# SwiGLU gate and up in a decoder trunk: the weight block in place of the tokens as the operand that is held

## The chip, the cores and the metric

The kernel runs on one core of one Trainium2 chip. The metric is the device time of one execution in microseconds (us). Shown is the median of three runs; a profile of one further execution says where the time goes. PE is TensorE (matmul), PEld its weight-load path, DVE VectorE, ACT ScalarE, POOL GpSimd, SP SyncE. A matmul has a stationary operand (up to 128 columns, loaded first) and a moving one (up to 512 columns); the columns of the stationary operand become the partitions of the result, and the moving columns lie along its free axis.

## The reference

The trunk has two layers over 256 tokens of width 1024. Each layer is feed-forward, token mixer (an RG-LRU block in the first layer, attention on a shared K and V in the second), feed-forward, each with a norm before and after. So there are four feed-forward parts (FFNs), and the change concerns them:

```python
def rms_norm(x, g):
    return x * lax.rsqrt(jnp.mean(x * x, axis=-1, keepdims=True) + EPS) * g

def swiglu(x, w_gate, w_up, w_down):            # 1024 -> 2816 -> 1024
    return (jax.nn.silu(x @ w_gate) * (x @ w_up)) @ w_down

f = swiglu(rms_norm(h, pre_g), w_gate, w_up, w_down)
h = h + 0.5 * rms_norm(f, post_g)
```

All inputs and the output are float32.

## The kernel before, in words

**Splitting.** Each float32 operand is split into an upper part that TensorE's fp32r format holds and the rest (`split`, lines 166 to 179: ACT writes `whi` at line 175, DVE writes `wlo` at line 176). Each product is three fp32r matmuls: upper by upper, upper by lower, lower by upper (`mm3`, lines 181 to 185).

**Items.** The work on weights is a list of items. An item's `prep` loads 512 KB of weights on SP's queue (`load_raw`, line 155; five buffers `raw`) and splits them (nine buffers each of `whi` and `wlo`); its `work` does the matmuls, once for each half t of the tokens (0 to 127 and 128 to 255). The function `run` (line 342) lets half 0 lead half 1 by 4 to 7 items; `slot` (line 333) does one piece and calls `tick`, which issues deferred work and prepares items ahead, when a running count of TensorE's work says that their load has landed.

**Gate and up** (`ffn_items`, line 453). For each of five blocks of 512 features, `proj_items` (line 357) makes four items for the gate and four for up. An item has two blocks k of 128 input features. For each k and t the stationary operand is the token block `xhi` or `xlo` (128 input features by 128 tokens), and 512 weight columns move. So the sums in PSUM (`mm`, four banks in turn) have tokens on partitions. `pair_items` (line 392) does the last 256 features of gate and up together. After a gate, ACT forms silu with the token's scale `rs[t]`, one number to a partition (line 467). After an up, DVE multiplies by silu and the scale into `prod` (line 476). Two ticks later `hidden_T` turns the product with four TensorE transposes (line 482), since the down projection needs features on partitions, and ACT and DVE split it into `hhi` and `hlo` (lines 486 and 487), one pair of tiles for each half.

**Down** (`row_items`, line 414): 22 items; the stationary operand is a block of `hhi` or `hlo`, 512 weight columns move, and two sums of 512 columns arise per half. `enter` (line 244) then normalizes, adds to the stream `h`, transposes it (line 214) and writes the next `xhi` and `xlo`; `stat` (line 239) finds the next scale `rs[t]`.

**Elsewhere.** The recurrent projection (`add_rec_units`, line 629) already holds weight blocks of 126 (the last 84) columns and moves all 256 tokens, through `mm3w` (lines 187 to 192). PE's instructions stand in the order in which they are written; the other engines' instructions are put in order by priority. Tiles lie in pools one behind another, so a tile's start depends on the sizes of those before it.

Of the kernel before, what the change touches and what calls it, by code (L numbers as in the profile page):

```python
# [9 lines left out]
F32 = mybir.dt.float32  # L10
# [6 lines left out]
P = 128  # L17
# [27 lines left out]
def trunk_kernel(ctx: ExitStack, tc: tile.TileContext, A: dict, out: bass.AP):  # L45
# [12 lines left out]
    def nm(s):  # L58
        uid[0] += 1
        return f"{s}_{uid[0]}"  # L60
# [78 lines left out]
    xhi = hpool.tile([P, 8, S], F32R, name="xhi")  # L139
    xlo = hpool.tile([P, 8, S], F32R, name="xlo")  # L140
# [96 lines left out]
    rs = [None, None]  # L237

    def stat(t):
        ss = new_ss()  # L240
        square_sum(h[t], ss[:, 0:1])
        rs[t] = rstd_of(ss, 1)

    def enter(t, dests, pf, gb, half, last=False, normed=False):

        f = 1.0 / 16 if half else 1.0 / 32
# [6 lines left out]
        for n in range(2):  # L253
            t1.append(hpool.tile([P, 512], F32, tag="t1", name=nm("t1"), bufs=2))
            nc.vector.tensor_tensor(t1[n], pf[n], gb[:, n * 512:(n + 1) * 512], ALU.mult)  # L255
        r = rstd_of(ss, 2, f)
# [9 lines left out]
        def inputs():  # L266
            tps = [to_tp(h[t], n) for n in range(2)]
            for dest in dests:
                to_x(tps, dest)
            stat(t)  # L270

# [181 lines left out]
    def ffn_items(pool_of, wg, wu, wd, post_g, next_dests, last=False, normed=False):  # L453
        hid = {}
        sil = {}
        box = {}

        def hid_tiles(t):
            if t not in hid:
                hid[t] = (pool_of().tile([P, 22, P], F32R, tag=f"hhi{t}", name=nm("hhi"), bufs=1),  # L460
                          pool_of().tile([P, 22, P], F32R, tag=f"hlo{t}", name=nm("hlo"), bufs=1))
            return hid[t]

        def post_gate(c0, nn):
            def f(t, ps):
                s = pool_of().tile([P, 512], F32, tag="sil", name=nm("sil"), bufs=2)
                nc.scalar.activation(s[:, :nn], ps, AF.Silu, scale=rs[t][:, 0:1])  # L467
                sil[t] = s
            return f

        def post_up(c0, nn):
            def f(t, ps):
                hh, hl = hid_tiles(t)
                s = sil[t][:, :nn]
                pr = pool_of().tile([P, 8 * HA], F32, tag="prod", name=nm("prod"), bufs=2)
                nc.vector.scalar_tensor_tensor(pr[:, :nn], ps, rs[t][:, 0:1], s, ALU.mult, ALU.mult)  # L476
                defer(HT, lambda: hidden_T(pr, hh, hl))

            def hidden_T(pr, hh, hl):
                tp = trbank()  # L480
                for j in range(nn // P):
                    nc.tensor.transpose(tp[:, j * P:(j + 1) * P], pr[:, j * P:(j + 1) * P], ident)  # L482
                k0 = c0 // P
                hv = hh[:, k0:k0 + nn // P, :].rearrange("p a b -> p (a b)")
                lv = hl[:, k0:k0 + nn // P, :].rearrange("p a b -> p (a b)")
                nc.scalar.activation(hv, tp[:, :nn], AF.Copy)  # L486
                nc.vector.tensor_tensor(lv, tp[:, :nn], hv.bitcast(F32), ALU.subtract)  # L487
# [7 lines left out]
        def post_both(t, pg, pu):  # L495
            post_gate(2560, 256)(t, pg)
            post_up(2560, 256)(t, pu)

        pair_items(wg, wu, 2560, 256, main_x, post_both)

        def load_gb():
            box["gb"] = gain_bcast(post_g)

        ahead(i0 + 24, load_gb)

        def post_down(t, accs):
            enter(t, next_dests(t), accs, box["gb"], True, last, normed)

        row_items(wd, [P] * 22, lambda t, k: (hid[t][0][:, k, :], hid[t][1][:, k, :]), post_down, 4 if last else 2)
        return i0  # L510

    def std_dests(gi):
        return lambda t: [main_dest(gi, t)]
# [37 lines left out]
    par = rw.tile([RT, NP], F32, name="par")  # L551
# [34 lines left out]
    ffn_items(lambda: pools["f"], A["ffn1_w_gate"][0], A["ffn1_w_up"][0], A["ffn1_w_down"][0], A["ffn1_post_g"][0],  # L586
# [262 lines left out]
    def dests_l1(t):  # L849
        zx[t] = (pools["f"].tile([P, 22, P], F32R, tag=f"hhi{t}", name=nm("zhi"), bufs=1),  # L850
                 pools["f"].tile([P, 22, P], F32R, tag=f"hlo{t}", name=nm("zlo"), bufs=1))
        return [(GI["kv"], zx[t][0][:, :8, :], zx[t][1][:, :8, :]), main_dest(GI[("ffn1", 1)], t)]

    ffn_items(lambda: pools["f"], A["ffn2_w_gate"][0], A["ffn2_w_up"][0], A["ffn2_w_down"][0], A["ffn2_post_g"][0], dests_l1)
    n_ffn2 = len(items)

    def kv_tiles():
# [5 lines left out]
        kv["bfb"] = lp.tile([P, NH], F32, name="bfb")  # L863
# [96 lines left out]
    for n in range(2):  # L960
        proj_items(A["w_kv"], n * 512, 512, z_x, post_k(n))

    ffn_items(lambda: pools["f"], A["ffn1_w_gate"][1], A["ffn1_w_up"][1], A["ffn1_w_down"][1], A["ffn1_post_g"][1],
              std_dests(GI[("mix", 1)]))
# [87 lines left out]
    for n in range(2):  # L1052
# [8 lines left out]
    ffn_items(lambda: pools["f"], A["ffn2_w_gate"][1], A["ffn2_w_up"][1], A["ffn2_w_down"][1], A["ffn2_post_g"][1],  # L1061
              lambda t: None, last=True)
# [77 lines left out]
    run(n_ffn1, lag_in=3, lag_out=8)  # L1140
# [24 lines left out]
    run(n_ffn2)  # L1165
    run(n_ffn3)
# [18 lines left out]
    run(len(items), lag_out=5)  # L1185
# [35 lines left out]
```

## Time and profile before

| | |
|---|---|
| median of 3 runs (lowest to highest) | 1015.52 us (1015.2 to 1015.7) |
| the profiled execution: span, first to last instruction | 1014.2 us |
| granted TensorE clock, mean share of full | 0.998 |
| weight splits (lines 175 and 176) | 329 on each of ACT and DVE, 342.7 and 395.6 us busy |
| transposes of the product (line 482) | 176 |
| DMA, mean over the span | 176 GB/s |

In the rows of groups the columns are: line, engine, operation, out<-in, shapes, count | busy us, mean ns of one | idle time of the engine just before. In rows in order of time they are: start us, duration us, engine, line, operation, out<-in, shapes, count. Rows of waits are: who waited <- for whom: us in total, times, longest. Rows of stretches are: stretch, length, then busy us and count for PE, PEld, DVE and ACT, then granted clock, DMA share and GB/s. Matmuls overlap in the pipeline: their durations do not add up to time.

### The profile page before, as it was taken

How to read it: one execution, taken by the hardware profiler on the slowest of the kernel's cores; microseconds unless marked ns; L12 is line 12 of the kernel's file. 1: busy time of each engine (PE TensorE's matmuls, PEld its weight loads, DVE VectorE, ACT ScalarE, POOL GpSimd, SP SyncE). 2: the span in 40 equal slices, each digit the busy share in tenths (PEclk: the TensorE clock that was granted, in tenths of full speed). 3: DMA queues.
4: the chain of work that ended last, by engine and by line, in shares of the span. 5: the costliest groups of instructions: out<-in, count | busy, mean ns of one | idle time of the engine just before them, and what ended most of it. 6: DMA issues, size and time to landing. Idle time of an engine off the chain costs nothing.

```text
span 1014.2 us, 12946 instructions
## 1 busy us (share of the span) xinstructions
PE 1001.5 (99%) x4826; PEld 832.0 (82%) x4826; DVE 608.8 (60%) x747; ACT 537.4 (53%) x737; POOL 47.2 (5%) x103
## 2 busy tenths in 40 slices
PE   8999999999999999999999999999999999999997
PEld 5788888889988888888898888888888888888885
DVE  4756554668998655554694555554477476555542
ACT  5645443559986544443564544444467565444431
POOL 1400000000003000000000000000010010000000
PEclk9999999999999999999999999999999999999999
DMA  6876555565337666555376666555445057665531
GB/s 228 288 232 203 190 184 187 166 180 153 123 98 228 203 191 178 195 186 169 114 251 197 177 184 187 185 182 186 164 167 167 1 192 222 177 196 187 184 107 42
DMA packets 91861, 178.85 MB, mean 176 GB/s; under 512 B 11790, under 2 KB 31318, under 8 KB 91798
## 3 DMA queue, kind: packets, MB, share of 16 engines
q1 hardware_dynamic: 90550, 176.89, 54.9%
q10 hardware_dynamic: 608, 1.06, 0.3%
q8 instruction: 38, 0.62, 0.2%
q0 software_dynamic: 640, 0.07, 0.1%
q14 instruction: 25, 0.20, 0.1%
HBM read 176.95 MB, written 1.05 MB: 176 GB/s over the span
## 4 chain that ended last, share of the span: by engine, by line
PE 89%; ACT 4%; DVE 3%; issue 1%; DMA 1%; POOL 1%; SPq 0%; DVEq 0%; POOLq 0%; ACTq 0%
PE mm L185 27%; PE mm L183 27%; PE mm L184 27%; PE tr L482 2%; PE gt L710 1%; DVE wlo L176 1%; PE mm L190 1%; PE mm L191 1%; PE mm L192 1%; PE gt L989 1%; PE mm L1016 1%; DMA raw<-in_ffn_w_gate_dram 1%; ACT junk L205 1%; PE gt L214 1%; PE tr L890 1%
## 5 line engine op out<-in xcount | busy, mean ns | idle before, releaser
L176 DVE TENSOR_TENSOR wlo<-raw,whi 128x1024 fp32r<-128x1024 f32 (+4 forms) x329 | 395.6, 1207 | 276.3 <-ACT whi L175 272.4
L175 ACT ACTIVATE whi<-raw 128x1024 fp32r<-128x1024 f32 (+4 forms) x329 | 342.7, 1046 | 320.6 <-PE mm L185 256.7
L183 PE MATMUL mm<-whi,xhi 128*128 128x512 f32 (+2 forms) x776 | 307.7, 397 | 0.1
L185 PE MATMUL mm<-whi,xlo 128*128 128x512 f32 (+2 forms) x776 | 302.1, 389 | 0.1
L184 PE MATMUL mm<-wlo,xhi 128*128 128x512 f32 (+2 forms) x776 | 301.5, 389 | 0.4 <-DVE wlo L1086 0.2
L185 PEld LDWEIGHTS mm<-whi,xlo 128*128 128x128 f32 x776 | 145.6, 188 | 31.4 <-DVE xlo L228 1.1
L184 PEld LDWEIGHTS mm<-wlo,xhi 128*128 128x128 f32 x776 | 146.0, 188 | 30.1 <-DVE wlo L176 1.2
L183 PEld LDWEIGHTS mm<-whi,xhi 128*128 128x128 f32 x776 | 145.8, 188 | 28.2 <-ACT xhi L223 0.5
L183 PE MATMUL mm<-whi,hhi 128*128 128x512 f32 x352 | 139.5, 396 | 0.0
L185 PE MATMUL mm<-whi,hlo 128*128 128x512 f32 x352 | 138.8, 394 | 0.0
L184 PE MATMUL mm<-wlo,hhi 128*128 128x512 f32 x352 | 138.5, 393 | 0.0
L185 PEld LDWEIGHTS mm<-whi,hlo 128*128 128x128 f32 x352 | 66.1, 188 | 15.4
L184 PEld LDWEIGHTS mm<-wlo,hhi 128*128 128x128 f32 x352 | 66.2, 188 | 15.1
L183 PEld LDWEIGHTS mm<-whi,hhi 128*128 128x128 f32 x352 | 66.1, 188 | 14.8
L476 DVE SCALAR_TENSOR_TENSOR prod<-mm,rstd,sil 128x512 f32<-128x512 f32 (+1 forms) x48 | 33.9, 706 | 41.5 <-PE mm L185 37.8
L467 ACT ACTIVATE sil<-mm,rstd 128x512 f32<-128x512 f32 (+1 forms) x48 | 31.3, 653 | 42.0 <-PE mm L185 42.0
L198 POOL TENSOR_SCALAR nv<-ss 128x1 f32<-128x1 f32 x24 | 10.4, 434 | 785.4 <-ACT junk L205 785.3
L486 ACT ACTIVATE hhi<-tr 128x512 fp32r<-128x512 f32 (+1 forms) x48 | 26.6, 554 | 15.4 <-PE tr L482 15.3
L255 DVE TENSOR_TENSOR t<-mm,gb 128x512 f32<-128x512 f32 x24 | 16.3, 689 | 30.0 <-ACT junk L205 29.9
L205 ACT ACTIVATE junk<-mm 128x512 bf16<-128x512 f32 x24 | 14.2, 592 | 34.2 <-PE mm L185 34.2
L487 DVE TENSOR_TENSOR hlo<-tr,hhi 128x512 fp32r<-128x512 f32 (+1 forms) x48 | 30.5, 643 | 1.4
L183 PE MATMUL mm<-whi,zhi 128*128 128x340 f32 (+2 forms) x80 | 28.5, 357 | 0.0
(177 smaller groups left out, 912.5 us busy)
## 6 DMA issues: line engine op xcount, KB each, us to landing
raw<-in_ffn_w_down_dram SPq DMA_DIRECT2D x88, 512.0 KB
raw<-in_ffn_w_up_dram SPq DMA_DIRECT2D x80, 512.0 KB
raw<-in_ffn_w_gate_dram SPq DMA_DIRECT2D x79, 512.0 KB
raw<-in_rg_w_in_dram SPq DMA_DIRECT2D x20, 504.0 KB
raw<-in_rg_w_out_dram SPq DMA_DIRECT2D x10, 504.0 KB
raw<-in_ffn_w_gate_dram SPq DMA_DIRECT2D x18, 256.0 KB
raw<-in_ffn_w_up_dram SPq DMA_DIRECT2D x16, 256.0 KB
raw<-in_w_kv_dram SPq DMA_DIRECT2D x8, 512.0 KB
```

The source lines that it names most:

```text
L175: nc.scalar.activation(hi[:parts, c:c + m], rawv[:, c:c + m], AF.Copy)
L176: nc.vector.tensor_tensor(lo[:parts, c:c + m], rawv[:, c:c + m], hi[:parts, c:c + m].bitcast(F32), ALU.subtract)
L183: nc.tensor.matmul(ps, xh, wh, start=first, stop=False)
L184: nc.tensor.matmul(ps, xh, wl, start=False, stop=False)
L185: nc.tensor.matmul(ps, xl, wh, start=False, stop=last)
L205: nc.scalar.activation(junk[:, :src.shape[1]], src, AF.Square, scale=f, accum_out=acc)
L255: nc.vector.tensor_tensor(t1[n], pf[n], gb[:, n * 512:(n + 1) * 512], ALU.mult)
L467: nc.scalar.activation(s[:, :nn], ps, AF.Silu, scale=rs[t][:, 0:1])
L476: nc.vector.scalar_tensor_tensor(pr[:, :nn], ps, rs[t][:, 0:1], s, ALU.mult, ALU.mult)
L482: nc.tensor.transpose(tp[:, j * P:(j + 1) * P], pr[:, j * P:(j + 1) * P], ident)
L486: nc.scalar.activation(hv, tp[:, :nn], AF.Copy)
L487: nc.vector.tensor_tensor(lv, tp[:, :nn], hv.bitcast(F32), ALU.subtract)
```

## The change

A new helper holds a block of 128 weight columns and moves 256 tokens, at the new lines 198 to 200:

```diff
+    def mmj(ps, wh, wl, k, first, last):
+        tensor_work(3 * S)
+        nc.tensor.matmul(ps, wh, xhi[:, k, :], start=first, stop=False)
+        nc.tensor.matmul(ps, wh, xlo[:, k, :], start=False, stop=False)
+        nc.tensor.matmul(ps, wl, xhi[:, k, :], start=False, stop=last)
```

In `ffn_items`, the first `lead` blocks of 512 features stay as they were (one block in three of the FFNs, none in the third); the others and the last 256 features take the new form, with features on partitions, so the product needs no transpose:

```diff
+        def gate_rows(n, ps):
+            s = sil["j", n] = gate_tile()
+            v = s.rearrange("p (a b) -> p a b", a=2)
+            nc.vector.tensor_tensor(v, ps.rearrange("p (a b) -> p a b", a=2),
+                                    rcp["v"].unsqueeze(1).to_broadcast([P, 2, S]), ALU.mult)
+            nc.scalar.activation(s, s, AF.Silu)
+
+        def up_rows(n, ps, k0):
+            hh, hl = hid_tiles()
+            pr = prod_tile()
+            nc.vector.tensor_tensor(pr, ps, sil["j", n], ALU.mult)
...
+            nc.scalar.activation(hv, pv, AF.Copy)
+            nc.vector.tensor_tensor(lv, pv, hv.bitcast(F32), ALU.subtract)
+
+        def tile_items(w, c0, post):
...
+                    for j in range(2):
+                        for b in range(4):
+                            o = j * 512 + b * P
+                            mmj(acc["b"][b // 2][:, (b % 2) * S:(b % 2 + 1) * S], u.hi[:, o:o + P], u.lo[:, o:o + P],
+                                k0 + j, k0 + j + b % 2 == 0, k0 + j == 7 and b % 2 == 1)
+                        if j == 0:
+                            tick()
+                    if k0 == 6:
+                        for n in range(2):
+                            post(n, acc["b"][n])
...
         for i in range(5):
-            proj_items(wg, i * 512, 512, main_x, post_gate(i * 512, 512))
-            proj_items(wu, i * 512, 512, main_x, post_up(i * 512, 512))
+            if i < lead:
+                proj_items(wg, i * 512, 512, main_x, post_gate)
+                proj_items(wu, i * 512, 512, main_x, post_up(i * 512))
+            else:
+                tile_items(wg, i * 512, gate_rows)
+                tile_items(wu, i * 512, lambda n, ps, i=i: up_rows(n, ps, 4 * i + 2 * n))
-        pair_items(wg, wu, 2560, 256, main_x, post_both)
+        last_items(2560)
```

`last_items` loads 256 columns of gate and of up together, as `pair_items` did. A two-bank sum now holds 512 features by 256 tokens in each form. The scale of a token must lie along the free axis for the gate; two matmuls with the identity make such a row, copied to `rcp`. The up side leaves the scale out; it is put in after the down projection, in `enter`:

```diff
+        rf[t] = spool.tile([P, 1], F32, tag="rf", name=nm("rf"), bufs=4)
+        nc.gpsimd.tensor_scalar(rf[t], rs[t], 1.0 / 16, None, ALU.mult)
+
+    def rstd_rows():
+        tp = trbank()
+        for t in range(2):
+            nc.tensor.matmul(tp[:, t * P:(t + 1) * P], rs[t].to_broadcast([P, P]), ident, start=True, stop=True)
+        rcp["v"] = hpool.tile([P, 512], F32, tag="t1", name=nm("rrow"), bufs=2)[:, :S]
+        nc.scalar.activation(rcp["v"], tp[:, :S], AF.Copy)
...
-        f = 1.0 / 16 if half else 1.0 / 32
+        f = rf[t][:, 0:1] if half else 1.0 / 32
+        r_in = rs[t][:, 0:1] if half else None
...
-            nc.vector.tensor_tensor(t1[n], pf[n], gb[:, n * 512:(n + 1) * 512], ALU.mult)
+            if half:
+                nc.vector.scalar_tensor_tensor(t1[n], pf[n], r_in, gb[:, n * 512:(n + 1) * 512], ALU.mult, ALU.mult)
```

The order of an FFN: the leading items run with their lag, the new items run with both halves at once, and the down items run again with a lag of four:

```diff
+    def run_ffn(ends, lag_out=LAG):
+        i1, i2, n = ends
+        if state["a"] < i1:
+            run(i1)
+        for i in range(i1, i2):
+            slot(None, i)
+        state["a"] = state["b"] = i2
+        run(n, MID, lag_out)
```

Tiles move. `xhi` and `xlo` become one tile in which the two alternate for each k; the hidden tiles hold both halves; and some pools get room that shifts what follows:

```diff
-    xhi = hpool.tile([P, 8, S], F32R, name="xhi")
-    xlo = hpool.tile([P, 8, S], F32R, name="xlo")
+    xall = hpool.tile([P, 8, 2, S], F32R, name="xall")
+    xhi, xlo = xall[:, :, 0, :], xall[:, :, 1, :]
...
-                hid[t] = (pool_of().tile([P, 22, P], F32R, tag=f"hhi{t}", name=nm("hhi"), bufs=1),
-                          pool_of().tile([P, 22, P], F32R, tag=f"hlo{t}", name=nm("hlo"), bufs=1))
+                for s in ("hhi", "hlo"):
+                    hid[s] = pool_of().tile([P, 2, 22, P], F32R, tag=s, name=nm(s), bufs=1)
...
-    par = rw.tile([RT, NP], F32, name="par")
+    par = rw.tile([RT, NP + 32], F32, name="par")[:, :NP]
...
+            rw.tile([P, 32], F32, name="pad")
...
-        kv["bfb"] = lp.tile([P, NH], F32, name="bfb")
+        kv["bfb"] = lp.tile([P, 2 * NH], F32, name="bfb")[:, :NH]
...
+        ap.tile([P, 32], F32, name="pad")
```

More of the change, by code (lines that the diff above doesn't have):

```diff
@@ L237, in trunk_kernel @@
     rs = [None, None]
+    rf = [None, None]
+    rcp = {}
     def stat(t):
@@ L471, in post_up, with hid_tiles @@
[L471 to L479, printed above, removed]
+        def hid_tiles():
+            if not hid:
+                for s in ("hhi", "hlo"):
+                    hid[s] = pool_of().tile([P, 2, 22, P], F32R, tag=s, name=nm(s), bufs=1)
+            return hid["hhi"], hid["hlo"]
@@ new lines, in gate_tile, with prod_tile, post_gate, post_up @@
+        def gate_tile():
+            return pool_of().tile([P, 512], F32, tag="sil", name=nm("sil"), bufs=2)
+        def prod_tile():
+            return pool_of().tile([P, 8 * HA], F32, tag="prod", name=nm("prod"), bufs=2)[:, :512]
+        def post_gate(t, ps):
+            s = sil[t] = gate_tile()
+            nc.scalar.activation(s, ps, AF.Silu, scale=rs[t][:, 0:1])
+        def post_up(c0):
+            def f(t, ps):
+                pr = prod_tile()
+                nc.vector.tensor_tensor(pr, ps, sil[t], ALU.mult)
+                defer(HT, lambda: hidden_T(pr, t))
+            def hidden_T(pr, t):
+                hh, hl = hid_tiles()
@@ new lines, in tile_items, with prep, work @@
+        def tile_items(w, c0, post):
+            acc = {}
+            for k0 in range(0, 8, 2):
+                def prep(k0=k0):
+                    return split(load_raw(w[k0 * P:(k0 + 2) * P, c0:c0 + 512].rearrange("(k p) n -> p k n", p=P), P, 1024),
+                                 P, 1024)
+                def work(t, u, k0=k0):
+                    if k0 == 0:
+                        acc["b"] = [mmbank(), mmbank()]
+                    for j in range(2):
[8 more added lines that the diff above has]
+                            post(n, acc["b"][n])
+                items.append((prep, work))
@@ new lines, in last_items, with prep, work @@
+        def last_items(c0):
+            acc = {}
+            for k0 in range(0, 8, 2):
+                def prep(k0=k0):
+                    raw = new_raw()
+                    v = raw.rearrange("p (k s n) -> p k s n", k=2, s=2)
+                    for s, w in enumerate((wg, wu)):
+                        nc.sync.dma_start(v[:, :, s, :], w[k0 * P:(k0 + 2) * P, c0:c0 + 256].rearrange("(k p) n -> p k n", p=P))
+                    return split(raw, P, 1024)
+                def work(t, u, k0=k0):
+                    if k0 == 0:
+                        acc["b"] = [mmbank(), mmbank()]
+                    for j in range(2):
+                        for b in range(4):
+                            o = j * 512 + b * P
+                            mmj(acc["b"][b // 2][:, (b % 2) * S:(b % 2 + 1) * S], u.hi[:, o:o + P], u.lo[:, o:o + P],
+                                k0 + j, k0 + j + b % 2 == 0, k0 + j == 7 and b % 2 == 1)
+                        if j == 0:
+                            tick()
+                    if k0 == 6:
+                        gate_rows(0, acc["b"][0])
+                        up_rows(0, acc["b"][1], c0 // P)
+                items.append((prep, work))
@@ L847, in trunk_kernel, with dests_l1 @@
     zx = [None, None]
[L849 to L855, printed above, removed]
+    def dests_l1(t, hid):
+        zx[t] = [hid[s][:, t, :8, :] for s in ("hhi", "hlo")]
+        return [(GI["kv"], *zx[t]), main_dest(GI[("ffn1", 1)], t)]
+    ffn_b = ffn_items(lambda: pools["f"], A["ffn2_w_gate"][0], A["ffn2_w_up"][0], A["ffn2_w_down"][0], A["ffn2_post_g"][0], dests_l1)
     def kv_tiles():
@@ L1164, in trunk_kernel @@
     fcm = open_pool("f", "ffn_b")
-    run(n_ffn2)
-    run(n_ffn3)
+    run_ffn(ffn_b)
+    run(n_kv)
+    run_ffn(ffn_c)
     fcm.__exit__(None, None, None)
@@ L1184, in trunk_kernel @@
     fcm = open_pool("f", "ffn_c")
-    run(len(items), lag_out=5)
+    run_ffn(ffn_d, 5)
     while pend or queue:
```

57 lines of the change are left out of this document (29 added, 28 removed).

## The prediction

> **What bounds the kernel now.** I read the clock, then the busy shares and the chain of waits, then the waits, and last the order of time on TensorE, stage by stage.
>
> ```profile
> core 0: 1014.2 us, clock 0.998
> ```
>
> ```profile
> span 1014.2 us, 12946 instructions
> ...
> PE 1001.5 (99%) x4826; PEld 832.0 (82%) x4826; DVE 608.8 (60%) x747; ACT 537.4 (53%) x737; POOL 47.2 (5%) x103
> ...
> PE 89%; ACT 4%; DVE 3%; issue 1%; DMA 1%; POOL 1%; SPq 0%; DVEq 0%; POOLq 0%; ACTq 0%
> ```
>
> ```profile
> ACT whi L175 <- PE mm L185: 256.7, 195, 3.1
> ACT sil L467 <- PE mm L185: 42.0, 43, 1.7
> DVE prod L476 <- PE mm L185: 37.8, 37, 1.8
> ```
>
> TensorE is bound at full clock (0.998): 99% busy, 89% of the chain. The other engines wait for it: the weight split for buffers that TensorE still reads, silu and product for its sums. So what the change is worth is the change in TensorE's own time, as long as nothing new comes late. Busy time alone does not give that time, because matmuls overlap: one shows 0.39 us but the next starts 0.23 us later. I therefore count **from start to start**. Gate and up of the first FFN, order of time (start, duration):
>
> ```profile
> 59.87 0.39 PE L183 MATMUL mm<-whi,xhi 128*128 128x512 f32 x1
> ...
> 65.31 0.39 PE L183 MATMUL mm<-whi,xhi 128*128 128x512 f32 x1
> ...
> 65.76 0.40 PE L185 MATMUL mm<-whi,xlo 128*128 128x512 f32 x1
> 66.00 0.60 PE L482 MATMUL tr<-ident,prod 128*128 128x128 f32 x4
> 66.36 0.47 PE L183 MATMUL mm<-whi,xhi 128*128 128x512 f32 x1
> 66.67 0.39 PE L184 MATMUL mm<-wlo,xhi 128*128 128x512 f32 x1
> ```
>
> From 59.87 to 65.31 there are 24 matmuls: 5.44/24 = 226.7 ns for one of 512 columns. From 65.76 to 66.67 there are two matmuls and four transposes: 0.91 - 2 x 0.2267 = 0.457 us, 0.114 us a transpose.
>
> **The kind of matmul that the change brings** is already in the trace: the recurrent projection (lines 190 to 192) holds a weight block and moves 256 tokens. One tile pair has blocks of 126 columns, the last one 84:
>
> ```profile
> 235.52 0.28 PE L190 MATMUL mm<-xhi,whi 128*126 128x256 f32 x1
> ...
> 240.81 0.28 PE L190 MATMUL mm<-xhi,whi 128*126 128x256 f32 x1
> ...
> 271.87 0.28 PE L190 MATMUL mm<-xhi,whi 128*84 128x256 f32 x1
> ...
> 273.97 0.28 PE L190 MATMUL mm<-xhi,whi 128*84 128x256 f32 x1
> ```
>
> 45 matmuls in 5.29 us are 117.6 ns each; with 84 columns 18 in 2.10 us, 116.7 ns. Two of 256 cost 235 where one of 512 costs 227: as it stands, this way of multiplying is 4% dearer.
>
> **Starts in memory.** The diff also moves tiles. In the built program before, the weight tiles whi and wlo and the inputs xhi and xlo start 160 bytes beyond a multiple of 256. The hidden tiles of FFN 1 start there too for tokens 0 to 127, but at 32 for tokens 128 to 255; those of the other three FFNs start at 96 and 224. Down projection of FFN 1 (the two token halves alternate every six matmuls), then of FFN 2:
>
> ```profile
> 160.05 0.39 PE L183 MATMUL mm<-whi,hhi 128*128 128x512 f32 x1
> ...
> 161.42 0.40 PE L183 MATMUL mm<-whi,hhi 128*128 128x512 f32 x1
> ...
> 162.82 0.39 PE L183 MATMUL mm<-whi,hhi 128*128 128x512 f32 x1
> ...
> 459.80 0.40 PE L183 MATMUL mm<-whi,hhi 128*128 128x512 f32 x1
> ...
> 462.59 0.40 PE L183 MATMUL mm<-whi,hhi 128*128 128x512 f32 x1
> ```
>
> The first six take 228.3 ns each, the next six 233.3, together 230.8; in FFN 2 the twelve take 232.5. The same shape takes 226.7 ns above, where both operands start at 160. I read this as: **equal starts of the block and of what moves are worth about 5.8 ns in 232.5**. After the change every hidden, attention-output and input tile starts at 160, and so does each block of 128 weight columns (512 bytes).
>
> **The change, part by part, on TensorE.**
>
> 1. *Gate and up.* Three FFNs keep their first 512 gate and up columns as before (8 items), then run 36 items in the new form; the third FFN runs all 44. That is 152 items, each 2 rows of blocks x 4 blocks x 3 = 24 matmuls of 256 columns in place of 12 of 512: 3648 for 1824. Before: 1824 x 226.7 ns = 413.5 us. After: 3648 x d. The trace has no 128-column block against 256 tokens from equal starts, so d has ends: 113.35 ns below (half of 226.7, cost by column alone) and 117.6 above (the row at lines 190 to 192, whose starts step by 504 and 1008 bytes and so mostly differ). I take that row, with the gain that equal starts show: 117.6 x 226.7/232.5 = 114.7 ns. 3648 x 114.7 = 418.4: **+4.9 us**. The ends are 0 and +15.5. "Held still" spares no load: two matmuls in a row with the same block have a load each, now and afterwards:
>
> ```profile
> L191 PEld LDWEIGHTS mm<-xlo,whi 128*126 128x126 f32 x80 | 14.9, 186 | 0.2
> ...
> L190 PEld LDWEIGHTS mm<-xhi,whi 128*126 128x126 f32 x80 | 14.9, 186 | 0.2
> ```
>
> The Trainium skill ("TensorE: Matmul & The Clock Gate", section "Back-to-back issue gap") speaks against more and shorter matmuls: a warm one takes N/2.4 ns plus about 2.5 ns that do not shrink with N. By it the spacings would be 109.2 and 215.8 ns and this term 398.4 - 393.6 = +4.8 us; the trace disagrees with both spacings (117.6 and 226.7 are 8 and 11 ns longer).
>
> 2. *Transposes.* 24 of 176 of line 482 stay: 152 x 0.114 = **-17.3 us**. The hidden split now reads the product from SBUF; ACT and DVE keep as many passes.
>
> 3. *Row of scales.* Features now lie on partitions, so the token's scale must lie along the free axis: two plain f32 matmuls of 128 columns, each run as two passes, at five places (the one after the third FFN is not used). The nearest row:
>
> ```profile
> 754.32 0.39 PE L185 MATMUL mm<-whi,xlo 128*128 128x512 f32 x1
> 754.55 1.05 PE L989 MATMUL gt<-kT,qT 66*128 66x128 f32 x8
> 755.36 0.47 PE L183 MATMUL mm<-whi,xhi 128*128 128x512 f32 x1
> 755.68 0.39 PE L184 MATMUL mm<-wlo,xhi 128*128 128x512 f32 x1
> ```
>
> Eight passes for 1.36 - 0.453 = 0.907 us, 0.113 each; 5 x 4 x 0.113 = **+2.3 us**.
>
> 4. *Equal starts in the down projections.* 264 matmuls an FFN: 3 x 264 x (232.5 - 226.7) = 4.6, and 264 x (230.8 - 226.7) = 1.1: **-5.7 us**. The ends are 0 and some 0.6 more from the key projection and attention output, which I leave out.
>
> 5. *Beside TensorE.* Each gate bank gets one more pass of DVE (38 in all), about what this row shows:
>
> ```profile
> L255 DVE TENSOR_TENSOR t<-mm,gb 128x512 f32<-128x512 f32 x24 | 16.3, 689 | 30.0 <-ACT junk L205 29.9
> ```
>
> 38 x 0.689 = 26 us on an engine that is 60% busy. It delays silu by 1.4 us, but the product that needs silu comes four items (11 us) later, and the gate's two banks are asked for again only then, after the up projection; without that cover each gate would cost 1.4 us, 24 us over the 17 full ones. Behind these passes on DVE stand weight splits for blocks some nine items away. The weight loads on SP are the same, in the same order. An item lasts 24 x 114.7 = 2.75 us, as before (12 x 226.7 = 2.72): no queue is pressed harder. The token halves no longer lag by 4 to 7 items inside these stretches; the lag is closed before them and opened after them on items whose inputs are long there: nothing lost, at most 1 us a seam (eight). The POOL multiply after each statistic and the per-token scale in the FFN's closing norm wait for nothing late: 0.
>
> Sum: 4.9 - 17.3 + 2.3 - 5.7 = **-15.8 us**. On the profiled span 1014.2 this is 998.4; the median of the runs, 1015.5, lies 1.3 above the span, so the forecast is **999.7 us**. Its own range is 993 to 1004 (d from 113.35 to 116). The point of no change is d = 113.35 + 20.7/3.648 = 119.0 ns.
>
> **Rivals.**
>
> *Equal starts do not help a 256-column stream.* Then d = 117.6: +15.5 - 17.3 + 2.3 - 5.7 = -5.2, **1010.3 us**. For it: the 84- and 126-column rows, of differing starts, are alike within 0.9 ns. Against it: the down rows above.
>
> *Starts are not the cause at all*, and the down rows have another reason: +15.5 - 17.3 + 2.3 = +0.5, **1016.0 us**, no change. Against it: halves that alternate within the same 3 us differ by 5 ns.
>
> *The load becomes the bound* (slower). In the 256-column stretch the load path never rests, in the 512-column one it does:
>
> ```profile
> 60.00:64.00 4.00, 4.00 (x20) 3.30 (x19) 0.53 (x1) 0.00 (x0) 1.00 0.79 267
> 236.00:241.00 5.00, 5.00 (x45) 5.00 (x44) 0.00 (x0) 0.59 (x1) 1.00 0.02 4
> ```
>
> (Second pair of columns: TensorE, then load path.) If a block of 128 and a stream from the same start then meet all the time, the 5.8 ns come on top: d = 123.4, +36.7 - 20.7 = +16.0, **1031.5 us**. It decides from d = 119.0. Against it: a load a third narrower (84 columns) gives the same spacing, so the load is not what paces now. The Trainium skill ("TensorE: Matmul & The Clock Gate", section "LDWEIGHTS (loading the stationary operand)") puts a load at P/1.2 ns, an estimate of 106.7 for 128 columns, under the stream; no row here shows it at this shape.
>
> *TensorE stands still* at the new seams or for gate banks (point 5): up to 24 + 8 us, 1032 us. Nothing in the order of instructions asks for it.
>
> **Chances.** Forecast 0.56; equal starts without effect on the new matmuls 0.26; no effect at all 0.06; load-bound 0.07; standing still 0.03; a spacing below half of 226.7 0.02. A measurement of this kernel can tell about 0.2% (2 us) from no change: faster 0.84, same 0.06, slower 0.10. The range 992 to 1012 takes in the forecast and the first rival and leaves out the rest.
>
> **What the changed profile would show.** Spacing at the new matmul lines near 115 ns (117.6 and 119 or more are the rivals); down projections at 227 ns in all FFNs; 24 transposes left; five short f32 groups; idle before TensorE still near nothing. I am wrong if the spacing passes 119 ns, or if TensorE waits for silu, products or banks.

## The result, and the profile after

The changed kernel takes **1019.08 us** (five runs, 1018.88 to 1019.87) against 1015.52 (1015.19 to 1015.7) for the kernel before: a ratio of 1.0037, 95% interval 1.0024 to 1.0049. It is slower by 3.6 us; forecast was 999.7 us, faster by 15.8. So the time is 19.4 us above the forecast. The profiled execution has a span of 1017.2 us, 3.0 above the 1014.2 of before.

The profile of the changed kernel, first its clock, then from its page the span, the busy shares and the chain that ended last:

```profile
core 0: 1017.2 us, clock 0.998
```

```profile
span 1017.2 us, 16436 instructions
...
PE 1004.2 (99%) x6518; PEld 915.0 (90%) x6518; DVE 628.3 (62%) x777; ACT 533.9 (52%) x734; POOL 52.7 (5%) x113
...
PE 90%; ACT 4%; DVE 4%; issue 2%; POOL 1%; DVEq 0%; POOLq 0%; ACTq 0%
```

Clock and busy share of TensorE are those of before, and its share of the chain is 90% in place of 89%. No engine has become late: TensorE's new lines stand still for nothing (the last number of their row), and the weight split still waits for TensorE and not the other way round. Busy time has grown on the load path, from 832 to 915 us, and by the additional passes on DVE, from 609 to 628. From the groups, then from the waits:

```profile
L198 PE MATMUL mm<-xall,whi 128*128 128x256 f32 x1216 | 344.7, 283 | 0.0
L198 PEld LDWEIGHTS mm<-xall,whi 128*128 128x128 f32 x1216 | 233.4, 192 | 0.2
```

```profile
ACT whi L175 <- PE mm L199: 207.9, 123, 1.9
ACT whi L175 <- PE mm L185: 131.2, 99, 3.5
```

So the loss lies inside the stream of matmuls. Order of time in a new stretch of the first FFN, start and duration first, and in the down projection of the second:

```profile
100.07 0.28 PE L198 MATMUL mm<-xall,whi 128*128 128x256 f32 x1
100.19 0.28 PE L199 MATMUL mm<-xall,whi 128*128 128x256 f32 x1
100.31 0.28 PE L200 MATMUL mm<-xall,wlo 128*128 128x256 f32 x1
...
102.95 0.28 PE L198 MATMUL mm<-xall,whi 128*128 128x256 f32 x1
```

```profile
459.82 0.39 PE L183 MATMUL mm<-whi,hhi 128*128 128x512 f32 x1
...
462.54 0.39 PE L183 MATMUL mm<-whi,hhi 128*128 128x512 f32 x1
```

From 100.07 to 102.95 there are 24 matmuls: **120.0 ns each**, where 114.7 was forecast and 119.0 was the point of no change. Over all 3648 the middle eight in ten show 120 again, with a mean of 120.2. The twelve of 512 columns in the second extract take 226.7 ns each, as forecast (232.5 before). The difference of the spans, counted from each matmul's start to the next one's start over both traces:

| on TensorE | forecast | measured |
|---|---|---|
| gate and up taken out, with their 152 transposes | -430.8 | -431.9 |
| 3648 matmuls put in | +418.4 | **+438.4** |
| row of scales | +2.3 | +1.9 |
| down projections (measured: with the key projection) | -5.7 | -5.3 |
| sum | -15.8 | +3.1 |

The rest of TensorE's work, -0.1, makes it the 3.0 of the spans. The whole miss is the second row, 20.0 us. (Below, "spacing" is this number: the mean from start to start over all such matmuls of the FFN or run named; a few of them stand in front of a transpose or a wait. In the excerpts it can be recalculated from first, last and count, which gives the steady stretch and so sometimes a little less.)

### The profile page after: what moved, and what is told of

Same layout as the page of the kernel before. It is cut to its first block, busy times and chain, and to the rows that moved or that the text cites. A ratio compares the mean times of both kernels' runs of the same rounds, so it can differ in the third digit from the quotient of the medians.

```text
span 1017.2 us, 16436 instructions
## 1 busy us (share of the span) xinstructions
PE 1004.2 (99%) x6518; PEld 915.0 (90%) x6518; DVE 628.3 (62%) x777; ACT 533.9 (52%) x734; POOL 52.7 (5%) x113
## 4 chain that ended last, share of the span: by engine, by line
PE 90%; ACT 4%; DVE 4%; issue 2%; POOL 1%; DVEq 0%; POOLq 0%; ACTq 0%
PE mm L198 14%; PE mm L200 14%; PE mm L199 14%; PE mm L185 13%; PE mm L184 13%; PE mm L183 13%; PE gt L815 1%; DVE wlo L176 1%; PE mm L190 1%; PE mm L191 1%; PE mm L192 1%; PE gt L1094 1%; PE mm L1121 1%; ACT junk L213 1%; PE gt L222 1%
## 5 line engine op out<-in xcount | busy, mean ns | idle before, releaser
L198 PE MATMUL mm<-xall,whi 128*128 128x256 f32 x1216 | 344.7, 283 | 0.0
L200 PE MATMUL mm<-xall,wlo 128*128 128x256 f32 x1216 | 344.1, 283 | 0.0
L199 PE MATMUL mm<-xall,whi 128*128 128x256 f32 x1216 | 344.1, 283 | 0.0
L198 PEld LDWEIGHTS mm<-xall,whi 128*128 128x128 f32 x1216 | 233.4, 192 | 0.2
L199 PEld LDWEIGHTS mm<-xall,whi 128*128 128x128 f32 x1216 | 233.4, 192 | 0.2
L200 PEld LDWEIGHTS mm<-xall,wlo 128*128 128x128 f32 x1216 | 233.4, 192 | 0.0
L183 PE MATMUL mm<-whi,hhi 128*128 128x512 f32 (+2 forms) x432 | 166.1, 384 | 0.0
L185 PE MATMUL mm<-whi,hlo 128*128 128x512 f32 (+2 forms) x432 | 165.0, 382 | 0.0
L184 PE MATMUL mm<-wlo,hhi 128*128 128x512 f32 (+2 forms) x432 | 164.9, 382 | 0.0
L183 PE MATMUL mm<-whi,xall 128*128 128x512 f32 (+2 forms) x168 | 67.1, 400 | 0.1
L184 PE MATMUL mm<-wlo,xall 128*128 128x512 f32 (+2 forms) x168 | 65.0, 387 | 0.4 <-DVE wlo L1191 0.2
L185 PE MATMUL mm<-whi,xall 128*128 128x512 f32 (+2 forms) x168 | 64.8, 386 | 0.1
L185 PEld LDWEIGHTS mm<-whi,xall 128*128 128x128 f32 x168 | 31.6, 188 | 7.0 <-DVE xall L236 1.1
L183 PEld LDWEIGHTS mm<-whi,xall 128*128 128x128 f32 x168 | 31.6, 188 | 5.7 <-ACT xall L231 0.5
```

What stands on the lines that cost most here:

```text
L183: nc.tensor.matmul(ps, xh, wh, start=first, stop=False)
L184: nc.tensor.matmul(ps, xh, wl, start=False, stop=False)
L185: nc.tensor.matmul(ps, xl, wh, start=False, stop=last)
L198: nc.tensor.matmul(ps, wh, xhi[:, k, :], start=first, stop=False)
L199: nc.tensor.matmul(ps, wh, xlo[:, k, :], start=False, stop=False)
L200: nc.tensor.matmul(ps, wl, xhi[:, k, :], start=False, stop=last)
```

## The experiments

The question was why a matmul of 256 columns, from equal starts, costs 120.0 ns and not 114.7. **Distance** below is the start of the tile that moves minus that of the block that is held, in bytes of a partition, modulo 256. In the changed kernel it is 0 for every matmul of gate and up. The theories on trial were: a fixed price of 13.3 ns beside the columns that every load brings (A; by these traces 256 columns more cost 226.7 - 120.0 = 106.7 ns, which leaves 13.3 of the 120.0); a load that paces at 120 ns by itself (B); equal starts that collide at 256 columns (C); and a pace that depends on the distance in a finer way (D).

### Inputs that start elsewhere for each k

```diff
-    xall = hpool.tile([P, 8, 2, S], F32R, name="xall")
+    xall = hpool.tile([P, 8, 2 * S + 8], F32R, name="xall")
```

Each of the eight input blocks starts 32 bytes further than the one before, so the eight distances alternate within every sum.

> The changed kernel, but the inputs of the eight input blocks k start 0, 32, 64, ... 224 bytes further than the weight blocks (mod 256). Read the start-to-start spacing of the new 256-column matmuls for each k. Theory A (a fixed price of 13.3 ns a matmul on top of 256 columns at 2.4 a ns): 120 ns at every k. Theory B (the 128-column load paces, 120 ns by itself): 120 ns at every k. Theory C (equal starts collide when the load path never rests): 120 ns at k = 0 only, 115 to 118 ns at most others; if so the time falls by about 3192 x 3 ns = 10 us.

Measured: 1014.07 us (one run; before, on the same chip, 1015.49). The mean spacing is 118.4 ns; by distance it lies between 117.5 (at 160; 117.6 at 192) and 119.1 (at 96), and at 0 it is 119.0: no distance shows 120 any more. The starts matter for this stream, and equal ones are worse than an even mixture. That speaks against A and B as the whole story. C did not come out as expected either: the time fell by 5.0 us in place of 10, and distance 0 is not set apart from the others.

### A narrower block

```diff
+        m, n = size if 0 < k < 7 else (P, S)
-        nc.tensor.matmul(ps, wh, xhi[:, k, :], start=first, stop=False)
+        nc.tensor.matmul(ps[:m, :n], wh[:, :m], xhi[:, k, :n], start=first, stop=False)
```

The same goes for the other two matmuls; `size` is (128, 256), (126, 256), (96, 256) and (64, 256) in the four FFNs.

> The changed kernel, but in the input blocks k = 1 to 6 of the new matmuls the weight block has 128, 126, 96 and 64 columns in the first, second, third and fourth FFN (the sums of the left-out features lack these blocks). Theory A: 120 ns at every width, or, if the price goes with the loaded columns, 120, 119.8, 116.7, 113.3. Theory B: 120, 118, then 107 to 113 (the stream alone) at 96 and 64. Theory C says nothing of its own beyond 117 where 126 columns no longer keep step.

Measured: 1009.9 us, and spacings of 120.4, 117.5, 116.2 and 113.6 ns for 128, 126, 96 and 64 columns. Groups of the load path in this kernel, then order of time in its fourth FFN:

```profile
L199 PEld LDWEIGHTS mm<-xall,whi 128*96 128x96 f32 x264 | 42.5, 161 | 0.0
...
L199 PEld LDWEIGHTS mm<-xall,whi 128*64 128x64 f32 x216 | 29.0, 134 | 0.0
```

```profile
899.80 0.28 PE L199 MATMUL mm<-xall,whi 128*64 128x256 f32 x1
...
902.52 0.28 PE L199 MATMUL mm<-xall,whi 128*64 128x256 f32 x1
```

With half the block, a load shows 134 ns in place of 192, and the 24 matmuls take 113.3 ns each. The price beside the columns shrinks with the load, so it is not the same for every width (A in its first form falls). But this run does not decide between the theories. A price that goes with the loaded columns was expected to give 120, 119.8, 116.7 and 113.3, and only 126 columns are clearly off it. B meets all but the 96 columns, where it expected 107 to 113, and C meets the 117 at 126. The next run decides against B, and the run with another start against both forms of A.

### Fewer tokens moved

```diff
+        m, n = size if k else (P, S)
-        nc.tensor.matmul(ps, wh, xhi[:, k, :], start=first, stop=False)
+        nc.tensor.matmul(ps[:m, :n], wh[:, :m], xhi[:, k, :n], start=first, stop=False)
```

The same for the other two, with 256, 224, 192 and 128 tokens in the four FFNs.

> The changed kernel, but in the input blocks k = 1 to 7 of the new matmuls only 256, 224, 192 and 128 tokens move in the first, second, third and fourth FFN (the sums of the other tokens lack these blocks). Theory A: 120, 106.7, 93.3, 66.7 ns. Theory B: 120 ns at every width. Theory C: near 120 for all as long as the load path has no rest.

Measured: 998.68 us; the spacing is 120 ns with 256 tokens and has a median of 111 for each of the three smaller numbers. Order of time in the second and the fourth FFN:

```profile
359.92 0.28 PE L199 MATMUL mm<-xall,whi 128*128 128x224 f32 x1
...
361.93 0.27 PE L199 MATMUL mm<-xall,whi 128*128 128x224 f32 x1
...
880.23 0.27 PE L199 MATMUL mm<-xall,whi 128*128 128x128 f32 x1
...
882.91 0.27 PE L199 MATMUL mm<-xall,whi 128*128 128x128 f32 x1
```

18 matmuls in 2.01 us and 24 in 2.68: 111.7 ns each, whether 224 or 128 columns move. So there is a floor of about 111 ns. It refutes B at 120, and also the 106.7 to 66.7 ns that A expected here and the 120 of C. I read it as the floor that the loads of 128 columns set; no run changed the load at these widths, so that is not shown. The Trainium skill ("TensorE: Matmul & The Clock Gate", section "LDWEIGHTS (loading the stationary operand)") puts a load at P/1.2 ns for P columns, an estimate of 106.7 for 128; the spacing here is about 5 ns above that. At 256 columns the stream stands 8 to 9 ns above this floor, so the load alone does not explain its 120.0 either.

### The old form with equal starts

The kernel before with nothing but room in two places, so that all hidden tiles start at 160 modulo 256 as the weights do:

```diff
-        kv["bfb"] = lp.tile([P, NH], F32, name="bfb")
+        kv["bfb"] = lp.tile([P, 2 * NH], F32, name="bfb")[:, :NH]
```

(and 16 floats more on the pools of `prod` and `htok`)

> The kernel before, with two small paddings only, so that all hidden, z and attention-output tiles start at 160 mod 256 like the weights; gate and up in the old form. If equal starts are what makes the down projection 227 instead of 232.5 ns: about 5.7 us less, 1009.8 us, ratio 0.9944. If the down gain in the changed kernel comes from something else (the joint tiles, the order): 1015.5 us, ratio 1.000.

Measured: 1010.42 us (five runs, 1010.29 to 1013.93; before 1015.49), ratio 0.9959 (0.9946 to 0.9973). Its down projection in the second FFN, order of time:

```profile
459.52 0.39 PE L183 MATMUL mm<-whi,hhi 128*128 128x512 f32 x1
...
462.24 0.39 PE L183 MATMUL mm<-whi,hhi 128*128 128x512 f32 x1
```

Twelve in 2.72 us, 226.7 ns. The realignment alone is worth 5.1 us; the fourth term (5.7) and the reading behind it stand, for 512 columns.

### One load for two moving tiles

```diff
-        nc.tensor.matmul(ps, wh, xhi[:, k, :], start=first, stop=False)
-        nc.tensor.matmul(ps, wh, xlo[:, k, :], start=False, stop=False)
+        nc.tensor.matmul(bank, wh, xall[:, k, :, :], start=first, stop=False)
         nc.tensor.matmul(ps, wl, xhi[:, k, :], start=False, stop=last)
```

`wh` meets the upper and the lower part of the inputs in one matmul of 512 columns; the kernel leaves out the separation of the sums, so those of two blocks run into each other.

> The changed kernel with the two products of a weight block's upper part (by the upper and by the lower inputs) made one matmul of 512 columns over the whole bank, so that a block has two loads in place of three; the sums of two blocks then run into each other, which leaves the amount of moved columns as it was. If every load of 128 columns costs the stream 13.3 ns (price per load): spacing 226.7 and 120, so 346.7 for 360 a block, 1216 x 13.3 = 16.2 us less than the changed kernel, 1002.9 us. If the cost goes with the moved columns (120/256 a column): 240 and 120, no change, 1019 us.

Measured: 1007.37 us (four runs; before 1015.23), ratio 0.9921 (0.9906 to 0.9935). Order of time:

```profile
100.09 0.40 PE L198 MATMUL mm<-xall,whi 128*128 128x512 f32 x1
100.32 0.28 PE L199 MATMUL mm<-xall,wlo 128*128 128x256 f32 x1
100.44 0.39 PE L198 MATMUL mm<-xall,whi 128*128 128x512 f32 x1
...
102.86 0.40 PE L198 MATMUL mm<-xall,whi 128*128 128x512 f32 x1
```

Eight blocks in 2.77 us; over the run 234.5 + 116.1 = 350.6 ns a block in place of 3 x 120.2 = 360.6, by FFN 348.5, 353.6, 347.3 and 353.5. Fewer loads do gain 11.7 us against the changed kernel, but less than the 16.2 of a fixed price for each. The same starts that give 120 in a pure stream of 256 give 116 here, and those that give 226.7 in a pure stream of 512 give 234: the pace belongs to the sequence, not to the single matmul. It also differs by 6 ns a block between FFNs whose distances are all 0.

### Another start for the inputs alone

The changed kernel with 48 floats of room before `xall` and 16 after it; together 256 bytes, so all else keeps its start modulo 256. The inputs then start at 96 modulo 256, the blocks at 160: distance 192.

```diff
+    hpool.tile([P, 48], F32, name="pad0")
     xall = hpool.tile([P, 8, 2, S], F32R, name="xall")
+    hpool.tile([P, 16], F32, name="pad1")
```

> The changed kernel with the inputs starting at 96 (mod 256) in place of 160, all else where it was. Price per load with a small part for the starts, as the blocks of e1_starts32 with 96 showed: spacing 117.2 ns in place of 120, 3648 x 2.8 = 10 us less, given back in part by the old-form matmuls that hold inputs (some 450 at 5.8 ns, 2.6 us): about 1011.5 us. If equal starts only lock the pace and any other fixed start locks it elsewhere, 113 to 120: 994 to 1019 us.

Measured: **1000.37 us** (four runs, 999.98 to 1000.58; before 1015.23), ratio 0.9851 (0.9835 to 0.9868). Nothing of the work differs from the changed kernel, and it is 18.7 us shorter. Order of time at the same place as above:

```profile
99.79 0.28 PE L200 MATMUL mm<-xall,whi 128*128 128x256 f32 x1
99.90 0.28 PE L201 MATMUL mm<-xall,whi 128*128 128x256 f32 x1
100.02 0.28 PE L202 MATMUL mm<-xall,wlo 128*128 128x256 f32 x1
...
102.51 0.28 PE L200 MATMUL mm<-xall,whi 128*128 128x256 f32 x1
```

24 in 2.72 us, 113.3 ns, half of the best pace of 512 columns; the mean over the run is 114.8. With the same columns and the same loads the spacing has fallen by 5.4 ns, which neither a price for each load (A) nor a load that paces (B) allows. By count, 3648 x (120.2 - 114.8) = 19.7 us, less what the leading blocks and the mixers lose, whose matmuls of 512 columns on held inputs go from a median of 227 ns to one of 229 to 231. Nothing but the start of the inputs has changed, so this start is the cause of the miss. The value that the expectation took from the alternating run (about 117) was too high for a stream that keeps one distance.

The start is not all that sets the pace, though. The spacing is 113.9, 113.5 and 113.5 ns in the first, second and fourth FFN, but 117.9 in the third, with the same distance of 192. Its beginning in order of time (L995 transposes the keys):

```profile
544.74 0.28 PE L200 MATMUL mm<-xall,whi 128*128 128x256 f32 x1
...
547.45 0.28 PE L202 MATMUL mm<-xall,wlo 128*128 128x256 f32 x1
547.57 0.60 PE L995 MATMUL tr<-ident,htok 128*66 128x128 f32 x4
...
548.60 0.28 PE L202 MATMUL mm<-xall,wlo 128*128 128x256 f32 x1
...
549.28 0.28 PE L202 MATMUL mm<-xall,wlo 128*128 128x256 f32 x1
549.40 0.60 PE L995 MATMUL tr<-ident,htok 128*66 128x128 f32 x4
...
556.90 0.28 PE L200 MATMUL mm<-xall,whi 128*128 128x256 f32 x1
...
559.73 0.28 PE L200 MATMUL mm<-xall,whi 128*128 128x256 f32 x1
```

Up to the first four transposes there are 23 steps in 2.71 us, 117.8 ns each. Between the two groups six steps take 0.68 us, 113.3 each, and after the second group 24 take 2.83, 117.9; the FFN keeps that pace for its remaining 1020 matmuls. The kernel of the last experiment shows the same three paces here. So at this distance the stream has two steady paces, and it can change from one to the other where it is interrupted; the other FFNs settle at 113.3 after each interruption. In the changed kernel, at distance 0, every long stretch settles at 120.0. What decides between the two paces is not known.

### The transposes alone

The old form from equal starts with the 176 transposes left out (the product is split as it stands, so the hidden values stand in the wrong order):

```diff
-            tp = trbank()
-            for j in range(nn // P):
-                nc.tensor.transpose(tp[:, j * P:(j + 1) * P], pr[:, j * P:(j + 1) * P], ident)
+            tp = pr
```

> The kernel before with equal starts (e4_old_form_equal_starts), with the 176 transposes of the product left out: the product is split as it stands, so the down projection reads it with tokens and features exchanged. If a transpose costs 0.114 us of TensorE time: 176 x 0.114 = 20 us less than that kernel's 1010.4, 990.3 us. If part of them hides behind a wait or a load: less than 20 us.

Measured: 989.38 us (four runs; before 1015.23), ratio 0.9745 (0.973 to 0.976); 21.0 us below the same kernel with them. Its page:

```profile
span 988.2 us, 12577 instructions
...
PE 975.3 (99%) x4650; PEld 814.8 (82%) x4650; DVE 606.5 (61%) x747; ACT 535.8 (54%) x737; POOL 47.8 (5%) x103
```

TensorE has 176 instructions fewer and is as busy as before, so nothing took their place: 21.0/176 = 0.119 us each, and the 152 of the change 18.1 us, an estimate. The second term (17.3) stands.

### Four distances in the new form, four in the old, four more in the new

The input tile is 64 floats longer, and each part of the trunk reads and writes it through a view shifted by a constant of its own:

```diff
+    xbig = hpool.tile([P, 8 * 2 * S + 64], F32R, name="xall")
+    SHIFT = {0: 8, 16: 0, 32: 16, 8: 32, 24: 0, 40: 56}
...
+        v = xbig[:, SHIFT[gi]:SHIFT[gi] + 16 * S].rearrange("p (k s n) -> p k s n", k=8, s=2)
```

The numbers are floats, in the order first FFN, first mixer, second FFN, third FFN, second mixer, fourth FFN; these give distances of 32, 64, 128 and 224 bytes to the FFNs. The second kernel does this in the old form from equal starts, with 32, 96, 160 and 224; there the weights move and the inputs are held, so the distances are 224, 160, 96 and 32. The third, in the new form, has 96, 160, 176 and 208.

> The changed kernel with the inputs of each FFN starting elsewhere: 32, 64, 128 and 224 bytes beyond the weight blocks (mod 256) in the first to fourth FFN, the mixers at 0. Theory D (the distance of the two starts sets where the pace locks): each FFN has a spacing of its own between 113.3 and 120 ns, steady within it; 0 gave 120 and 192 gave 113 to 114. Theory E (only equal starts are bad, any other is good): 113 to 115 in all four. Price per load: about 117 to 118 in all four, and 192 was a lucky one.

> The kernel before with equal starts (e4_old_form_equal_starts), with the held inputs of each FFN starting 32, 96, 160 and 224 bytes beyond equal in the first to fourth FFN (moving weights minus block: 224, 160, 96, 32). Theory D: a spacing of its own in each FFN, between 220 (213.3 and 6.7, what the best start leaves of 256 columns) and 233 ns. If equal starts are the best that 512 columns can have: 229 to 233 ns in all four, and about 2112 x 5 ns = 10 us more than 1010.4, some 1020 us.

> As e8_new_form_starts, with the inputs 96, 160, 176 and 208 bytes beyond the weight blocks (mod 256) in the first to fourth FFN. Theory D (the distance sets the pace): 117 to 119 ns at 96 and 160, like the other distances tried, and an answer to how narrow the good place at 192 is: below 116 at 176 and 208 if it is wide, 117 or more if it is narrow.

Measured: 1012.72, 1022.58 and 1017.7 us, one run each (before: 1015.41, 1015.41, 1015.87). The second FFN of the first kernel (distance 64), then the first FFN of the second (distance 224):

```profile
359.75 0.28 PE L207 MATMUL mm<-xall,whi 128*128 128x256 f32 x1
...
362.57 0.28 PE L207 MATMUL mm<-xall,whi 128*128 128x256 f32 x1
```

```profile
99.90 0.40 PE L192 MATMUL mm<-whi,xall 128*128 128x512 f32 x1
...
102.00 0.40 PE L192 MATMUL mm<-whi,xall 128*128 128x512 f32 x1
```

24 in 2.82 us are 117.5 ns, nine in 2.10 are 233.3. All runs together, spacing in ns by distance (the second row leaves out matmuls that waited):

| distance | 0 | 32 | 64 | 96 | 128 | 160 | 176 | 192 | 208 | 224 |
|---|---|---|---|---|---|---|---|---|---|---|
| 256 columns move | 120.2 | 117.0 | 117.9 | 120.3 | 118.8 | 118.7 | 119.4 | **113.5-113.9**, third FFN 117.9 | 119.3 | 118.4 |
| 512 columns move | **227** | 233.3 | 230-232 | 233.3 | 232 | 234.1 | - | 233 | - | 233.1 |

At 512 columns equal starts are the best place and all others cost 3 to 7 ns. The four distances tried for it are alike within 1 ns, so D's spacing of its own for each did not show there. At 256 columns equal starts are among the two worst, and 192 is the best place, in three FFNs of four. It looks narrow: at 176 and 208 no stretch between two interruptions shows less than 118.9. But 128 and 176 were tried in the third FFN alone, where 192 gives 117.9 too, so these two can be compared with 192 only there.

C is too simple (96 is as bad as 0), and so is the theory that only equal starts are bad, which expected 113 to 115 at the first four distances. The price for each load, which expected 117 to 118 there, comes close to them but misses 96 and 192. Of the theories D is left for 256 columns, and only in part: the distance matters, but one distance can have two paces. The weight blocks start at 160 in every stream of 128-column blocks, so the runs do not tell the distance from the start of the inputs by itself.

### The version that follows

The changed kernel with distance 192 for the FFNs' inputs and 0 for the mixers', and without the row of scales that nobody reads:

```diff
+    SHIFT = {0: 48, 16: 0, 32: 48, 8: 48, 24: 0, 40: 48}
...
-            if t == 1:
+            if t == 1 and dests[-1][0] != GI[("mix", 1)]:
```

> The changed kernel with the inputs of the four FFNs starting 192 bytes beyond the weight blocks, as in e6_other_start, the inputs of the two mixers at equal starts again, and without the row of scales that nobody uses after the third FFN. Theory D: e6_other_start's 1000.4, less about 0.8 us in the mixers and 0.5 for the row: 999 us, ratio 0.984. If the start of the inputs matters only by chance of the layout: between 1000 and 1019 us.

Measured: **999.65 us** (five runs, 999.47 to 999.83; before 1015.41), ratio 0.9845 (0.9832 to 0.9859). It beats both kernels. From the kernel with another start for all inputs it can't be told apart, as the intervals overlap. Its clock line, page and a new stretch in order of time:

```profile
core 0: 998.0 us, clock 0.999
```

```profile
span 998.0 us, 16426 instructions
...
PE 984.6 (99%) x6514; PEld 895.0 (90%) x6514; DVE 625.6 (63%) x777; ACT 533.7 (53%) x733; POOL 51.5 (5%) x113
```

```profile
99.96 0.28 PE L207 MATMUL mm<-xall,whi 128*128 128x256 f32 x1
...
102.68 0.28 PE L207 MATMUL mm<-xall,whi 128*128 128x256 f32 x1
```

113.3 ns in this stretch, 114.8 as a mean, on an engine as busy as it ever was. The third FFN settles at 117.8 ns again; at 113.3 its last 1020 matmuls would take some 4.6 us less, an estimate.

## Why the prediction was wrong

**What bounds the kernel: right.** TensorE was and is 99% busy at full clock, and no engine, queue or seam became late. The rival in which TensorE stands still did not happen.

**Gate and up, first term: the step that failed.** It took the row at 117.6 ns "with the gain that equal starts show", 117.6 x 226.7/232.5 = 114.7. The gain had been seen at 512 moved columns only and was carried to 256 by proportion. The runs show that it doesn't carry over at all: 3648 matmuls at 120.2 ns cost +24.9 us where +4.9 was taken. At 256 columns equal starts are one of the two worst places (120.2), 2.6 ns above the row from which they were to take 2.9. That is 20.0 us; the other terms and the rest of TensorE's work err by 1.2 in all to the other side, which leaves the 18.8 by which the profiled span missed (1017.2 for 998.4). The term's upper end, 117.6, was also wrong as an end: the row on which it rested alternated among distances, and an average over places, as the run with eight distances is too (118.4), bounds no single one of them. (The lower end of its own range, 993 us, is by its own terms 994 to 995; nothing hangs on that.) That the kernel with another start has a mean of 114.8, next to the 114.7 of the forecast, is chance: it mixes 113.3 and 117.8, at starts that are not equal.

**The rival that came closest in kind** was the load-bound one: slower, and decided from 119.0. Its point of decision was right, its mechanism was not. It had the load path as the pace and the difference of the starts on top, for 123.4 ns. With fewer tokens moved the floor is 111, and a narrower block does not bring the spacing down in proportion. The argument used against this rival, that a load of 84 columns gives the same spacing as one of 126, compared two rows of mixed distances; at distance 0 the spacing does fall with the block, 120.4 to 113.6.

**"Equal starts do not help"** (1010.3) was right that they do not help at 256 columns, but took them as neutral; they cost 2.6 ns above its 117.6, some 9.5 us. **"Starts are not the cause"** (1016.0) lies nearest in number, by luck: its spacing was as much too low, and it left out the gain of the down projections. It is refuted: moving the inputs by 192 bytes of distance is worth 18.7 us, and the hidden tiles' move 5.1 us.

**Transposes, second term: right**: 17.3 forecast, 18.1 by the run without them. **Row of scales, third: right**: 2.3 forecast, 1.9 measured. One group in the changed kernel, order of time:

```profile
30.81 0.61 PE L260 MATMUL tr<-ident,rstd 128*128 128x128 f32 x4
```

**Down projections, fourth: right** in size (5.7, measured 5.3 and alone 5.1) and in cause. **Beside TensorE, fifth: right** at 0. The additional passes on DVE in the changed kernel last what the row of before said (689 ns), and no matmul waits for them:

```profile
L521 DVE TENSOR_TENSOR sil<-mm,rrow 128x512 f32<-128x512 f32 x38 | 26.1, 690 | 0.7 <-PE mm L200 0.2
```

**The rule weighed there.** The estimate by the Trainium skill ("TensorE: Matmul & The Clock Gate", section "Back-to-back issue gap") was +4.8 us for this term, close to the +4.9 that was taken. Neither came true, and that they agreed was no support for either. The section gives N/2.4 + 2.5 ns as the gap of an isolated matmul, and says that in a stream of loads and matmuls both set the spacing. The estimate of 109.2 ns that follows for 256 columns is in no run with full blocks here, the lowest of which show 113.3.

**What stays open** is why the start acts as it does: why the best place is at 192 for 256 columns and at 0 for 512, why the order of lengths changes both (one load for two tiles), and what makes a stream settle at 117.8 or at 113.3 ns at the same distance. The runs give the table, not the mechanism; whether the loads and the moving reads meet in the same part of the memory was not measured by itself. Distances that are no multiple of 16 bytes were not tried by themselves, and most places of the table were measured in one FFN of one run.

## What to carry to other kernels

On an engine that is 99% busy, a spacing measured at one shape is no price for another: before a forecast scales it, find a row with that width, that block and those starts, or give the number both signs. Read the spacing by stage, too: a mean over four FFNs hid that one of them ran at another pace. A change of tile order is also a change of addresses, so measure it from more than one start before you judge it: the same program ran at 1019.1 and at 1000.4 us with 48 floats of room between. And when one change holds several edits, run its parts apart; here the room for the hidden tiles (-5.1 us) and the missing transposes (-18.1) were good all along, and one start hid both.

## What the runs showed of the hardware that was not expected

- The spacing of these fp32r matmuls, each with a load of its own, changes with the start of one operand against the other's, modulo 256 bytes: 113.5 to 120.3 ns at 256 moved columns, 227 to 234 at 512, with the best place at a distance of 192 for the one and at 0 for the other. The blocks' start was the same throughout, so distance and start of the inputs are not told apart.
- At one distance a stream can hold either of two paces: at 192 the third FFN ran 24 matmuls at 117.8 ns, after four transposes 113.3, and after four more 117.8 for the remaining 1020.
- With 128 loaded columns the spacing stays at about 111 ns, however few columns move (224, 192 or 128); with 64 loaded columns and 256 moved it is 113.6.
- A transpose of 128 x 128 float32 in the stream costs 0.119 us, as much as a matmul of 256 columns of fp32r.
- Matmuls of 512 and 256 columns in turn take 350.6 ns a pair (347 to 354 by FFN), not the 226.7 + 120.2 = 346.9 of the two pure streams.
